# Stacking the high and low parts of prompt queries and keys by transfers inside SBUF

## The chip, the cores and the metric

One Trainium2 chip, one core of it, one launch. The metric is device time in microseconds (us) of one execution, as the median of the runs shown. The engines are PE (matrix products), DVE (vector), ACT (scalar, functions), POOL and SP; SP here only issues transfers, ACT issues some too.

## The reference

One inference step of a two-layer decoder on 1024 prompt tokens and eight samples of eight tokens. The change touches layer 0's differential attention on the prompt alone. There each of eight heads has two components (c) of 64 dimensions, with queries and keys normalised per component:

```python
q = rms_norm(zq.reshape(b, l, H_A, 2, DH_A), q_g) * (DH_A ** -0.5)
k = rms_norm(zk.reshape(b, l, H_A, 2, DH_A), k_g)
...
s = jnp.einsum('bqhcd,bkhcd->bhcqk', q, k).astype(jnp.float32)
bias = rel_bias[t5_bucket(q_pos[:, None] - k_pos[None, :])]
s = s + jnp.transpose(bias, (2, 0, 1)).astype(jnp.float32)[None, :, None]
...
p = jax.nn.softmax(s, axis=-1)
a = p[:, :, 0] - lam * p[:, :, 1]
return jnp.einsum('bhqk,bkhe->bqhe', a.astype(v.dtype), v)
```

Before it stands an input projection of 1024 to 7168 columns; after it, in the same layer, a spatial-gating branch and an output projection; then layer 1, a gated linear attention. All is float32 to within the tolerance of the comparison.

## The kernel before

The stage that the change is in runs over units, 8 heads (h) of 9 token blocks (i): eight prompt blocks of 128 tokens and one block of the 64 sample tokens. Its loop (lines 482 to 504) writes, for a step s, the work of several units at different ages: the projection `qkv_tile` of unit s, `qk_trans` of the unit two steps older, `scores` of the one five steps older, `av`, `av2` and `otrans` of still older ones. The order on each engine is not this one: the program is built with a scheduler that places every instruction by a modelled time line, within what the tiles' buffers and the dependences allow, and fixes the order engine by engine. On the chip each engine then runs its list in order, and an instruction that waits holds up those behind it on its engine.

Products in full precision are made from pairs: a value is rounded to a matmul format (the high part) and the difference to the value is the low part. For the projection three products are summed (lines 145 to 150), 24 matmuls of 384 columns for a prompt block; the 64 sample tokens stack both parts in one operand and need 16.

For the scores the same is done by stacking. `qk_trans` transposes a block's 128 columns of q and of k on PE into one PSUM tile `tp` (name qkt): its partitions 0 to 63 are component 0, 64 to 127 component 1. Per component c it then fills two SBUF tiles, `qs` (128 partitions; for c two sets of 128 columns, the high and the low part of q) and `ks` (128 partitions; for c the columns of four blocks). In `ks` the component's own 64 partitions hold the high part of k and the other 64 the low part; in `qs` both halves hold the same, the high part in the first set of columns and the low part in the second. So a score is two matmuls over 128 partitions in place of four over 64 (lines 391 to 396). `own` and `oth` are the component's own half and the other.

Before, DVE makes the high and low parts of q and k in five 64-partition steps per component, of which one, the copy of both q parts to the other half, is ACT's: 8 instructions on DVE and 2 on ACT for each unit. In the table PRM, 'qh': 'd' and 'kh': 'd' name DVE and 'qd': 'a' names ACT for these (line 92 is ACT's copy in the helper, lines 94 and 96 DVE's). 'qhb': 2 gives `qs` two buffers, 'ksb': 3 gives `ks` three, and 'qkb': 3 gives three to `qk`, the normalised rows that are transposed and, for k, also written out (line 354, on SP). The softmax has lines 402 to 415: DVE adds a bias band and takes the maximum, ACT exponentiates (409), DVE combines the components (415). Line 424 transposes the weights, line 431 multiplies them by v, lines 435 and 436 write and square the result on ACT, 443 transposes it (otp) and ACT stores that with a scale (oT). Transposes and v products share three PSUM buffers; the projection has one, which ACT empties into `qk` and `v`.

SP's queue carries the projection's weights (line 177, eight 192 KB loads per head into four buffers), the input rows, the key rows going out, one write per head of oT, and, once, sixteen small transfers of a bias table inside SBUF (line 232), in steps 20 to 27 of the loop as written.

Of the kernel before, what the change touches and what calls it, by code (L numbers as in the profile page):

```python
# [11 lines left out]
F32R = mybir.dt.float32r  # L12
I32 = mybir.dt.int32
AF = mybir.ActivationFunctionType
ALU = mybir.AluOpType
# [9 lines left out]
P = 128  # L25
KT = D // P
H = 8
DH = 64
# [6 lines left out]
TAU = 16.0  # L35
CH = ((0, 384), (384, 384), (768, 320))
NPRE = 8
PRM = {'ktc': 'a', 'ev': 'p', 'ekm': 'p', 'qem': 'd', 'gm': 2, 'wp': (3, 6), 'at': 'a', 'LQ': 2, 'LS': 5, 'LA': 6, 'L2': 8, 'LO': 12, 'on': 'a', 'oT': 'a', 'qk4': 'p', 'kh': 'd', 'vt': 'a', 'qkc': 'a', 'sq': 'p', 'kg': 'p', 'at0': 'a', 'at1': 'a', 'qh': 'd', 'onm': 'd', 'TS': True, 'p0': 2, 'p1': 2, 'qkb': 3, 'qhb': 2, 'ksb': 3, 'lpq': 2, 'qd': 'a', 'vb': 16, 'atb': 2, 'onb': 4}
ON = (0, 3, 6)
QB = 3  # L40
QE = 2
# [21 lines left out]
def rows(i):  # L63
    return P if i < NT - 1 else NS
# [12 lines left out]
def hybrid_step(  # L77
# [7 lines left out]
    nc = tc.nc  # L85
    pe, act, dve, pool = nc.tensor, nc.scalar, nc.vector, nc.gpsimd
# [3 lines left out]
    def cpy(e, o, i_, scale=None):  # L90
        if e == 'a':
            act.activation(o, i_, AF.Copy, scale=scale) if scale is not None else act.copy(o, i_)  # L92
        elif scale is not None:
            G[e].tensor_scalar_mul(o, i_, scale)
        else:
            G[e].tensor_copy(o, i_)

    def f32(a):
        return a.bitcast(F32)
# [88 lines left out]
    if True:  # L188
# [24 lines left out]
        def bias_setup(pp, ps, tb):  # L213
            rel = pp.tile([33, H], F32, name="rel", bufs=1)
            r31 = pp.tile([32, H], F32, name="r31", bufs=1)
            oh = pp.tile([33, 384], F32, tag="on", name="oh", bufs=PRM["onb"])
            dve.memset(rel[32:33, :], BIG)
# [5 lines left out]
            pe.matmul(bps[:H, :384], rel, oh, start=True, stop=True)  # L223
            bsb = pp.tile([H, 384], F32, tag="on", name="bsb", bufs=PRM["onb"])
            dve.tensor_copy(bsb, bps[:H, :384])
# [32 lines left out]
        with ExitStack() as p1:  # L258
            pa = p1.enter_context(tc.tile_pool(name="pa", bufs=2))
# [3 lines left out]
            kg = const([P, P], "kg")  # L263
            qg = const([P, 1], "qg")
# [5 lines left out]
            def small_consts():  # L270
                nc.sync.dma_start(kg, k_norm_g.rearrange("o c d -> o (c d)").broadcast_to([P, P]))
                nc.sync.dma_start(qg, q_norm_g.rearrange("o c d -> (o c d)")[:, None])
                nc.sync.dma_start(sg, subln_g.rearrange("o d -> d o"))
                lamt = pa.tile([P, 4, DH], F32, tag="p0", name="lamt", bufs=PRM["p0"])
                nc.sync.dma_start(lamt, lam.rearrange("o f d -> o (f d)").broadcast_to([P, 4 * DH]).rearrange("p (f d) -> p f d", f=4))
                nc.sync.dma_start(n1g, norm1_g.rearrange("o (k p) -> p (o k)", p=P))
                lamp = pa.tile([P, 2, DH], F32, tag="p0", name="lamp", bufs=PRM["p0"])
                lams = const([P, 2], "lams")
# [79 lines left out]
            def qk_trans(h, i, qk):  # L358
                r = rows(i)
                tp = ps.tile([P, 512], F32, tag="t", name=f"qkt{h}_{i}", bufs=3)  # L360
                pe.transpose(tp[:, 0:r], qk[:r, 0:128], ident[:r, :r])
                pe.transpose(tp[:, 128:128 + r], qk[:r, 128:256], ident[:r, :r])
                if i == NT - 1:
                    for c in range(2):
                        q8 = slice(c * DH, (c + 1) * DH)
                        act.activation(qbd[q8, h, :, h // 4, c, :], tp[q8, 0:NS].rearrange("p (b q) -> p b q", b=NB),
                                       AF.Copy, scale=qg[q8])
                    dve.tensor_copy(ksT[:, h, :], tp[:, 128:128 + NS])
                    return None
                qs = pa.tile([P, 2, 2, P], F32R, tag="qs", name=f"qs{h}_{i}", bufs=PRM["qhb"])  # L370
                if i % KW == 0:
                    kts[h, i // KW] = pa.tile([P, 2, KW * P], F32R, tag="ks", name=f"ks{h}_{i}", bufs=PRM["ksb"])
                ks = kts[h, i // KW]
                o = i % KW * P
                for c in range(2):
                    own, oth = slice(c * DH, (c + 1) * DH), slice((1 - c) * DH, (2 - c) * DH)
                    cpy(PRM['qh'], qs[own, c, 0], tp[own, 0:128], qg[own])
                    dve.scalar_tensor_tensor(qs[own, c, 1], tp[own, 0:128], qg[own], f32(qs[own, c, 0]), ALU.mult, ALU.subtract)  # L378
                    cpy(PRM['qd'], qs[oth, c], f32(qs[own, c]))
                    cpy(PRM['kh'], ks[own, c, o:o + P], tp[own, 128:256])  # L380
                    dve.tensor_tensor(ks[oth, c, o:o + P], tp[own, 128:256], f32(ks[own, c, o:o + P]), ALU.subtract)  # L381
                return (qs,)

            def scores(h, i, qs):
# [68 lines left out]
            wp = ps.tile([P, 512], F32, tag="t", name="wp", bufs=3)  # L453
# [28 lines left out]
            for s in range(len(units) + max(8, PRM['LO'] + 1)):  # L482
# [15 lines left out]
                if s < len(units):  # L498
                    h, i = units[s]
# [168 lines left out]
        with ExitStack() as p2:  # L668
            pb = p2.enter_context(tc.tile_pool(name="pb", bufs=1, reuse_waits="tile"))
            vb = [pb.tile([P, D], F32, name=f"vb{i}") for i in range(NT)]  # L670
# [218 lines left out]
    with ExitStack() as p4:  # L889
# [130 lines left out]
        for n, (c0, cw) in enumerate(CH):  # L1020
            tp = psd.tile([P, 512], F32, tag="x", name=f"rbp{n}", bufs=4)
            for q in range(3):
                i = n * 3 + q
# [390 lines left out]
        i = NT - 1  # L1414
# [5 lines left out]
        for n, i in enumerate(OO):  # L1420
            to = TO + PB * n + DO[n]
# [72 lines left out]
```

## Time and profile before

| | |
|---|---|
| median of 3 runs | 1789.59 us (1786.38 to 1795.03) |
| the profiled execution | 1789.87 us, its span 1788.1 us |
| PE busy | 1742.9 us, 97% of the span |
| DVE, ACT, POOL busy | 1006.3, 754.5, 605.6 us |
| transfers | 211.55 MB |

An engine's busy time is the union of its instructions' times. Matmuls overlap one another on PE, so their shown lengths add up to more than their pace. A row "x <- y L378: 2.2, 6, 0.6" in the waits says who waited for whom, for how many us in total, how often, and the longest. SP runs nothing but issues; its rows show how long an issue occupies the queue, and an arrow to a DMA on another engine's row shows when a transfer had landed for its reader.

### The profile page before, as it was taken

To read this page: it belongs to the slowest core of one execution; us is meant where nothing else is said; L and a number is where in the kernel's file an instruction comes from. 1 tells how busy PE (TensorE), PEld (TensorE's weight loads), DVE (VectorE), ACT (ScalarE), POOL (GpSimd) and SP (SyncE) were. 2 spreads that over 40 slices of the span, in tenths; PEclk is the share of its full clock that TensorE was granted. 3 is DMA by queue.
4 is the path that set the end of the run, shared out by engine and by line. 5 is a ranking of instruction groups with operands and counts; after the bars stand their busy time and mean duration, and the time that the engine had idled before them with its cause. 6 is when DMAs were issued, how large, how long until landed. Compare 5 with 4: busy or idle time off the path is not lost.

```text
span 1788.1 us, 31862 instructions
## 1 busy us (share of the span) xinstructions
PE 1742.9 (97%) x11437; PEld 1631.3 (91%) x11437; DVE 1006.3 (56%) x2231; ACT 754.5 (42%) x1934; POOL 605.6 (34%) x881
## 2 busy tenths in 40 slices
PE   8999999999999999999999999999899999998998
PEld 8898999999999888889999999999899999996777
DVE  6988988888892322324833442534265445667442
ACT  5666666665763222223222332423252334345241
POOL 5656655565653221011522100144012223235240
PEclk8999999999999999999999999999999999998999
DMA  7202211220223766747221362433134334438741
GB/s 212 59 20 75 68 42 45 68 67 19 67 71 121 244 218 216 242 142 221 72 77 60 109 188 74 134 94 92 59 121 144 101 119 125 129 116 264 239 127 71
DMA packets 223141, 211.55 MB, mean 118 GB/s; under 512 B 22253, under 2 KB 200982, under 8 KB 222982
## 3 DMA queue, kind: packets, MB, share of 16 engines
q1 hardware_dynamic: 203350, 194.29, 35.1%
q10 hardware_dynamic: 19632, 15.21, 2.8%
q8 instruction: 91, 1.49, 0.4%
q14 instruction: 68, 0.56, 0.1%
HBM read 151.29 MB, written 56.24 MB: 116 GB/s over the span
## 4 chain that ended last, share of the span: by engine, by line
PE 66%; DVE 15%; DMA 6%; ACT 5%; POOL 4%; issue 3%; SPq 0%; ACTq 0%; POOLq 0%; DVEq 0%
PE o L1371 5%; PE yo L148 3%; PE yo L150 3%; PE yo L149 3%; PE vg L148 3%; PE vg L149 3%; PE vg L150 3%; PE zv L148 2%; PE zu L148 2%; PE zv L149 2%; PE zv L150 2%; PE zu L150 2%; PE gb L148 2%; PE zu L149 2%; PE gb L149 2%
## 5 line engine op out<-in xcount | busy, mean ns | idle before, releaser
L409 ACT ACTIVATE p<-s,nm 128x256 f32<-128x256 f32 (+7 forms) x128 | 95.0, 747 | 44.5 <-DVE nm L406 26.1
L396 PE MATMUL s<-ks,qs 128*128 128x512 f32 (+3 forms) x384 | 95.6, 363 | 3.9 <-DVE ks L381 2.2
L92 ACT CAST qs<-qs 64x256 fp32r<-64x256 f32 x128 | 51.7, 404 | 83.5 <-DVE qs L378 77.6
L1118 POOL TENSOR_TENSOR e<-e,k 128x256 f32<-128x256 f32 (+1 forms) x50 | 42.2, 850 | 111.6 <-ACT e L1115 97.6
L396 PEld LDWEIGHTS s<-ks,qs 128*128 128x128 f32 x384 | 64.3, 189 | 14.3 <-ACT qs L92 3.8
L431 PE MATMUL o<-v,at 128*128 128x128 f32 x576 | 75.9, 277 | 1.4 <-ACT at L92 1.4
L136 POOL TENSOR_TENSOR s<-s,mhalf 128x4 f32<-128x4 f32 (+1 forms) x72 | 74.5, 1035 | 5.2
L335 POOL TENSOR_TENSOR sq<-qk 128x256 f32<-128x256 f32 (+1 forms) x72 | 47.8, 664 | 83.1 <-ACT qk L92 82.1
L431 PEld LDWEIGHTS o<-v,at 128*128 128x128 f32 x576 | 70.6, 192 | 4.0 <-ACT at L92 2.4
L834 DVE TENSOR_TENSOR yp<-yp,yo 128x384 f32<-128x384 f32 (+1 forms) x48 | 25.4, 530 | 75.6 <-ACT yp L833 41.7
L404 DVE TENSOR_REDUCE nm<-s 128x1 f32<-128x640 f32 (+3 forms) x64 | 65.2, 1019 | 1.1
L744 POOL TENSOR_TENSOR u<-u,th 128x384 f32<-128x384 f32 (+1 forms) x24 | 28.6, 1192 | 99.8 <-DVE th L743 99.3
L402 DVE TENSOR_TENSOR s<-s,tb 128x256 f32<-128x256 f32 (+1 forms) x128 | 52.5, 412 | 8.9 <-PE s L396 5.8
L415 DVE SCALAR_TENSOR_TENSOR p<-p,fac,p 128x128 f32<-128x128 f32 (+3 forms) x64 | 54.7, 854 | 1.6
L1371 PE MATMUL o<-w1h,oh 128*128 128x512 f32 x128 | 53.0, 414 | 1.2 <-ACT oh L1348 1.2
L92 ACT COPY at<-atp 128x512 f32<-128x512 f32 (+2 forms) x96 | 44.6, 480 | 14.7 <-PE atp L424 14.2
L1371 PE MATMUL o<-w1l,oh 128*128 128x512 f32 x128 | 50.8, 397 | 0.0
L1371 PE MATMUL o<-w1h,ol 128*128 128x512 f32 x128 | 50.3, 407 | 0.0
L743 DVE SCALAR_TENSOR_TENSOR th<-th,gb 128x384 f32<-128x384 f32 (+1 forms) x24 | 12.5, 526 | 65.3 <-ACT th L742 65.3
L424 PE MATMUL atp<-cf,p 128*128 128x128 f32 x288 | 46.7, 273 | 1.7 <-DVE p L415 1.4
L340 POOL TENSOR_TENSOR qk<-qk,s 128x256 f32<-128x256 f32 (+1 forms) x72 | 46.0, 638 | 4.5
L1115 ACT ACTIVATE e<-e 128x512 f32<-128x512 f32 (+1 forms) x50 | 31.1, 623 | 37.4 <-DVE e L1114 33.6
(819 smaller groups left out, 6344.2 us busy)
## 6 DMA issues: line engine op xcount, KB each, us to landing
kp<-in_cache_k SPq DMA_DIRECT2D x32, 512.0 KB
vp<-in_cache_v SPq DMA_DIRECT2D x32, 512.0 KB
or<-oT_d SPq DMA_DIRECT2D x16, 384.0 KB
vb_d<-zs SPq DMA_DIRECT2D x36, 128.0 KB
oT_d<-ob SPq DMA_DIRECT2D x8, 544.0 KB
gt<-g_d SPq DMA_DIRECT2D x34, 128.0 KB
xt<-in_x_prompt SPq DMA_DIRECT2D x8, 512.0 KB
out<-v ACTq DMA_DIRECT2D x64, 64.0 KB
```

What stands on the lines that cost most here:

```text
L92: act.activation(o, i_, AF.Copy, scale=scale) if scale is not None else act.copy(o, i_)
L136: pool.tensor_tensor(dst, dst, mhalf[:dst.shape[0], :n], ALU.pow)
L148: pe.matmul(out, lh, rh, start=(s == 0), stop=False)
L149: pe.matmul(out, lh, rl, start=False, stop=False)
L150: pe.matmul(out, ll, rh, start=False, stop=(s == n - 1))
L396: pe.matmul(sc[c][:, k0:k0 + w], qs[:, c, l], kts[h, j][:, c, :w], start=(l == 0), stop=(l == 1))
L402: dve.tensor_tensor(sc[c][:, lo:n], sc[c][:, lo:n], backwards(tb[:, h, 0:n - lo]), ALU.add)
L404: dve.tensor_reduce(nm[:, c:c + 1], sc[c][:, :n], axis=AX.X, op=ALU.max, negate=True)
L409: act.activation(pc[:, :n], sc[c][:, :n], AF.Exp, bias=nm[:, c:c + 1], accum_out=ss[:, c:c + 1])
L415: dve.scalar_tensor_tensor(pt[0][:, :n], pt[1][:, :n], fac, pt[0][:, :n], ALU.mult, ALU.add)
L431: pe.matmul(op[:, :P], at[:, j * P:(j + 1) * P], vts[h, j], start=(j == 0), stop=(j == i))
L1371: pe.matmul(it.mp[:r], lh[:, k, :r], rh[k][:, cs], start=(k == 0 and a == 0), stop=(k == KT - 1 and a == 2))
```

## The change

For a unit the PSUM tile is now written by instructions on all 128 partitions into one SBUF tile `sp`, which has one buffer: on ACT the scaled high part of q and the high part of k, on DVE both low parts. Then SP issues eight transfers inside SBUF, each on 64 partitions: for each component and each half of the partitions, one of 128 columns from `sp` to `ks` and one of 256 columns from `sp` to `qs`. `qk` has two buffers in place of three.

```diff
-PRM = {..., 'qkb': 3, 'qhb': 2, 'ksb': 3, ...}
+PRM = {..., 'qkb': 2, 'qhb': 2, 'ksb': 3, ...}
...
                 o = i % KW * P
+                sp = pa.tile([P, 2, 2, P], F32R, tag="sp", name=f"sp{h}_{i}", bufs=1)
+                act.activation(sp[:, 0, 0], tp[:, 0:128], AF.Copy, scale=qg)
+                act.copy(sp[:, 1, 0], tp[:, 128:256])
+                dve.scalar_tensor_tensor(sp[:, 0, 1], tp[:, 0:128], qg, f32(sp[:, 0, 0]), ALU.mult, ALU.subtract)
+                dve.tensor_tensor(sp[:, 1, 1], tp[:, 128:256], f32(sp[:, 1, 0]), ALU.subtract)
                 for c in range(2):
-                    own, oth = slice(c * DH, (c + 1) * DH), slice((1 - c) * DH, (2 - c) * DH)
-                    cpy(PRM['qh'], qs[own, c, 0], tp[own, 0:128], qg[own])
-                    dve.scalar_tensor_tensor(qs[own, c, 1], tp[own, 0:128], qg[own], f32(qs[own, c, 0]), ALU.mult, ALU.subtract)
-                    cpy(PRM['qd'], qs[oth, c], f32(qs[own, c]))
-                    cpy(PRM['kh'], ks[own, c, o:o + P], tp[own, 128:256])
-                    dve.tensor_tensor(ks[oth, c, o:o + P], tp[own, 128:256], f32(ks[own, c, o:o + P]), ALU.subtract)
+                    own = slice(c * DH, (c + 1) * DH)
+                    for u in range(2):
+                        to = slice(u * DH, (u + 1) * DH)
+                        nc.sync.dma_start(f32(ks[to, c, o:o + P]), f32(sp[own, 1, u]))
+                        nc.sync.dma_start(f32(qs[to, c]), f32(sp[own, 0]))
                 return (qs,)
```

The scheduler then places everything of the stage anew. Three places show how. In these rows qs5_1 is the tile of head 5, block 1, and so on; the last number only counts.

SP's queue before, in head 4, where the key rows of blocks 1 to 4 go out one after another (each row with the semaphores that it waits for):

```order
L354 DMA out_2<-qk4_1_3898 128x128 [waits DMAHW6_49,Activation_49,Pool_49]
L354 DMA out_2<-qk4_2_4001 128x128 [waits DMAHW0_49,Activation_49,Pool_49]
L354 DMA out_2<-qk4_3_4157 128x128 [waits DMAHW2_49,Activation_49,Pool_49]
L354 DMA out_2<-qk4_4_4241 128x128 [waits DMAHW4_49,Activation_49,Pool_49]
L354 DMA out_2<-qk4_5_4332 128x128 [waits DMAHW6_49,Activation_49,Pool_49]
```

SP's queue now, in head 5, between the key rows of blocks 2 and 3:

```order
L354 DMA out_2<-qk5_2_5017 128x128 [waits DMAHW4_49,Pool_49]
L384 DMA ks5_0_4978<-sp5_1_5090 64x128 [waits DMAHW6_49,Activation_49]
L384 DMA ks5_0_4978<-sp5_1_5090 64x128 [waits DMAHW7_49]
L385 DMA qs5_1_5089<-sp5_1_5090 64x256 [waits DMAHW0_49,DVE_49,PE_49]
L384 DMA ks5_0_4978<-sp5_1_5090 64x128 [waits DMAHW1_49,DVE_49]
L385 DMA qs5_1_5089<-sp5_1_5090 64x256 [waits DMAHW2_49]
L385 DMA qs5_1_5089<-sp5_1_5090 64x256 [waits DMAHW3_49]
L384 DMA ks5_0_4978<-sp5_1_5090 64x128 [waits DMAHW4_49]
L385 DMA qs5_1_5089<-sp5_1_5090 64x256 [waits DMAHW5_49]
L354 DMA out_2<-qk5_3_5176 128x128 [waits DMAHW6_49,Pool_49]
```

Between two key rows there are now the eight transfers of an older block; the first needs ACT's part only, the third DVE's and the score matmuls that last read this qs buffer.

ACT's list before, around block 1 of head 5:

```order
L92 CAST qs5_1_4966<-qs5_1_4966 64x256
L92 COPY qk5_3_5050<-qkv5_3_5025 128x256
L92 COPY v5_3_5060<-qkv5_3_5025 128x128
L92 ACTIVATE oT4_4908<-otp4_1_5064,sg_115 128x128
L355 DMA out_3<-v5_3_5060 128x128
L92 CAST qs5_1_4966<-qs5_1_4966 64x256
L92 ACTIVATE on4_5_5074<-o4_5_5067,rr4_5_4755 128x128
```

And now at the same block:

```order
L92 COPY v5_3_5186<-qkv5_3_5151 128x128
L92 ACTIVATE oT4_5031<-otp4_1_5190,sg_115 128x128
L376 ACTIVATE sp5_1_5090<-qkt5_1_5086,qg_114 128x128
L377 CAST sp5_1_5090<-qkt5_1_5086 128x128
L355 DMA out_3<-v5_3_5186 128x128
L92 ACTIVATE on4_5_5200<-o4_5_5193,rr4_5_4875 128x128
L440 ACTIVATE osq4_5_5201,ms4_5_5202<-o4_5_5193,rr4_5_4875 128x128
```

The two copies from DVE's parts have become two writes from PSUM, which stand together, behind the store of a transposed output and before the next output.

PE's list before, where head 5's scores of block 0 (second component) and block 1 (first component) stand, with the value products of head 4's block 5 between them:

```order
L396 MATMUL s_0_5167<-ks_0_4858,qs_0_4857 128x128 x2
L443 MATMUL otp_1_5064<-cf,on_1_4602 128x128
L431 MATMUL o_5_5067<-v_0_3812,at_5_4818 128x128
L431 MATMUL o_5_5067<-v_1_3908,at_5_4818 128x128
L431 MATMUL o_5_5067<-v_2_4011,at_5_4818 128x128
L431 MATMUL o_5_5067<-v_3_4167,at_5_4818 128x128
L431 MATMUL o_5_5067<-v_4_4251,at_5_4818 128x128
L431 MATMUL o_5_5067<-v_5_4342,at_5_4818 128x128
L396 MATMUL s_1_5263<-ks_0_4858,qs_1_4966 128x256 x2
```

And now there:

```order
L447 MATMUL otp_1_5190<-cf,on_1_4719 128x128
L400 MATMUL s_0_5296<-ks_0_4978,qs_0_4977 128x128 x2
L435 MATMUL o_5_5193<-v_0_3908,at_5_4938 128x128
L435 MATMUL o_5_5193<-v_1_4004,at_5_4938 128x128
L435 MATMUL o_5_5193<-v_2_4110,at_5_4938 128x128
L435 MATMUL o_5_5193<-v_3_4269,at_5_4938 128x128
L435 MATMUL o_5_5193<-v_4_4356,at_5_4938 128x128
L435 MATMUL o_5_5193<-v_5_4450,at_5_4938 128x128
L400 MATMUL s_0_5296<-ks_0_4978,qs_0_4977 128x128 x2
```

Block 0's two components now enclose the value products, and block 1's first stands behind the next projection; the transpose otp, on which ACT's store before sp5_1 waits, stands just ahead of block 0's scores.

## Rows read from the trace of the kernel before

**Rows 1.** The page: busy time by engine, and DVE in 40 slices, in tenths.

```profile
PE 1742.9 (97%) x11437; PEld 1631.3 (91%) x11437; DVE 1006.3 (56%) x2231; ACT 754.5 (42%) x1934; POOL 605.6 (34%) x881
DVE  6988988888892322324833442534265445667442
```

**Rows 2.** Busy time over five stretches, 50 to 550 us: their sum.

```profile
sum 500.00, PE 485.65 PEld 458.84 DVE 437.54 ACT 321.33 POOL 292.50; mean PE 97.13 PEld 91.77 DVE 87.51 ACT 64.27 POOL 58.50
```

**Rows 3.** Time line of PE in head 3: start, length, engine, line, operation, count.

```profile
251.99 0.38 PE L424 MATMUL atp<-cf,p 128*128 128x128 f32 x2
...
253.42 0.33 PE L148 MATMUL qkv<-wq3h,xh 128*128 128x384 f32 x1
253.59 0.33 PE L149 MATMUL qkv<-wq3l,xh 128*128 128x384 f32 x1
...
257.42 0.39 PE L431 MATMUL o<-v,at 128*128 128x128 f32 x2
```

**Rows 4.** Time line of ACT's queue: one issue per head, three heads apart.

```profile
325.97 0.50 ACTq L325 DMA_DIRECT2D sx<-st  x1
...
515.59 0.50 ACTq L325 DMA_DIRECT2D sx<-st  x1
```

**Rows 5.** Waits to 560 us on PE and its weight load; SP's over the span.

```profile
PE s L396 <- DVE ks L381: 2.2, 6, 0.6
...
PE qkt L361 <- DVE ks L381: 1.7, 4, 0.9
...
PEld s L396 <- ACT qs L92: 3.8, 7, 0.7
...
SPq L354 <- POOL qk L341: 272.1, 64, 5.7
```

**Rows 6.** Groups to 620 us: shapes, count, busy us, mean ns, idle before, releaser.

```profile
L404 DVE TENSOR_REDUCE nm<-s 128x1 f32<-128x640 f32 (+3 forms) x64 | 65.2, 1019 | 1.1
...
L378 DVE SCALAR_TENSOR_TENSOR qs<-qkt,qg,qs 64x128 fp32r<-64x128 f32 x128 | 44.5, 348 | 3.6
L94 DVE TENSOR_SCALAR qs<-qkt,qg 64x128 fp32r<-64x128 f32 x128 | 44.3, 346 | 1.9
L381 DVE TENSOR_TENSOR ks<-qkt,ks 64x128 fp32r<-64x128 f32 x128 | 36.9, 289 | 4.1
L96 DVE CAST ks<-qkt 64x128 fp32r<-64x128 f32 x128 | 36.1, 282 | 0.0
...
L94 DVE TENSOR_SCALAR on<-on,ms 128x128 f32<-128x128 f32 x64 | 25.3, 396 | 14.8 <-POOL ms L136 13.6
...
L92 ACT CAST qs<-qs 64x256 fp32r<-64x256 f32 x128 | 51.7, 404 | 83.5 <-DVE qs L378 77.6 <-DVE fac L414 3.6
...
L92 ACT ACTIVATE oT<-otp,sg 128x128 f32<-128x128 f32 x64 | 23.9, 377 | 0.6 <-PE otp L443 0.4
...
L92 ACT COPY v<-qkv 128x128 f32<-128x128 f32 x64 | 17.3, 271 | 0.1
```

**Rows 7.** Time line, later stages: 64-partition transfers inside SBUF and their readers.

```profile
1272.49 0.50 SPq L940 DMA_DIRECT2D vsx<-vst  x1
1274.65 0.51 DVE L954 TENSOR_TENSOR vst<-vst,vsx 64x344 f32<-64x344 f32 x1 [2.24 <-DMA vsx<-vst]
...
1732.55 0.48 ACTq L1367 DMA_DIRECT2D ysx<-yr  x1
1735.20 0.68 DVE L1379 TENSOR_TENSOR yr<-yr,ysx 64x512 f32<-64x512 f32 x1 [0.64 <-DMA ysx<-yr]
```

**Rows 8.** Time line of SP's queue in head 0: issues in a row are merged.

```profile
45.45 0.37 SPq L354 DMA_DIRECT2D out<-qk  x1
45.87 2.65 SPq L232 DMA_DIRECT2D biasS<-tb  x4
...
49.05 7.10 SPq L232 DMA_DIRECT2D biasS<-tb  x10
```

More of the change, by code (lines that the diff above doesn't have):

```diff
@@ L37 @@
 NPRE = 8
-PRM = {'ktc': 'a', 'ev': 'p', 'ekm': 'p', 'qem': 'd', 'gm': 2, 'wp': (3, 6), 'at': 'a', 'LQ': 2, 'LS': 5, 'LA': 6, 'L2': 8, 'LO': 12, 'on': 'a', 'oT': 'a', 'qk4': 'p', 'kh': 'd', 'vt': 'a', 'qkc': 'a', 'sq': 'p', 'kg': 'p', 'at0': 'a', 'at1': 'a', 'qh': 'd', 'onm': 'd', 'TS': True, 'p0': 2, 'p1': 2, 'qkb': 3, 'qhb': 2, 'ksb': 3, 'lpq': 2, 'qd': 'a', 'vb': 16, 'atb': 2, 'onb': 4}
+PRM = {'ktc': 'a', 'ev': 'p', 'ekm': 'p', 'qem': 'd', 'gm': 2, 'wp': (3, 6), 'at': 'a', 'LQ': 2, 'LS': 5, 'LA': 6, 'L2': 8, 'LO': 12, 'on': 'a', 'oT': 'a', 'qk4': 'p', 'kh': 'd', 'vt': 'a', 'qkc': 'a', 'sq': 'p', 'kg': 'p', 'at0': 'a', 'at1': 'a', 'qh': 'd', 'onm': 'd', 'TS': True, 'p0': 2, 'p1': 2, 'qkb': 2, 'qhb': 2, 'ksb': 3, 'lpq': 2, 'qd': 'a', 'vb': 16, 'atb': 2, 'onb': 4}
 ON = (0, 3, 6)
```

## The prediction

> **What bounds the kernel now.** I read the page first, then the stretches, the groups by line, the waits, and last the time lines of SP and PE. The page gives PE 97% and DVE 56% of the span [rows 1], but DVE's slices show two regimes: mostly eight or nine tenths in the first twelve, mostly two to four afterwards [rows 1]. The edited lines run only in that first part, eight heads of eight prompt blocks and one sample block. In its 500 us from 50 to 550 PE is busy 485.7, DVE 437.5 and ACT 321.3 [rows 2], so what PE can visibly get back there is 14.3 us. A little more is hidden in it, since matmuls overlap. Projection matmuls of 384 columns start 0.17 us apart (0.173 over a longer run; two of the starts stand in [rows 3]), though each is shown 0.33 long; two transposes take 0.38, the first of which ends at 0.27, so they start 0.11 apart, and so do the fp32 halves of the value product [rows 3]. One head has 208 projection matmuls (8 blocks of 24, and 16 of the sample block), 48 score matmuls on 18,432 columns, 62 transposes and 72 value-product records: 36.0 + 8.3 + 6.8 + 8.1 = 59.2 us. A head lasts (515.59 - 325.97)/3 = 63.2 us [rows 4]. So PE sets the pace of this stage, it loses 4.0 us per head or 32 in all, and that is the ceiling of any gain (1.8%). Of PE's visible waits, those ended by the lines under edit are 2.2 + 1.7 on PE and 3.8 on its weight load, 7.7 us [rows 5]. ACT waits 77.6 us for DVE inside the edited lines [rows 6], and that wait is not on PE's path.
>
> **What is removed.** Per block DVE loses two each of 346, 348, 282 and 289 ns: 2.53 us; ACT loses two of 404: 0.81 us [rows 6]. The new instructions work on 128 partitions with the same 128 columns. Rows nearby with 128x128 cost what 64x128 costs: the scaled write of the attention output 377 ns on ACT against 404 for 64x256, the value copy 271, and DVE's 128x128 scaling 396 against 346 [rows 6]. I take 0.38 + 0.27 = 0.65 us on ACT and 0.35 + 0.29 = 0.64 on DVE (the two subtracting rows as they stand). DVE saves 1.9 us per block, 121 us over 64 blocks, ACT 10 us. Both engines work beside PE, so this is worth only what PE waits for them: 7.7 us by the rows that name the chain, 32 at the ceiling. I take **-8**; the gain would come near the ceiling only if all of PE's other waits were DVE's too.
>
> **What is added.** SP issues eight transfers per block, 512 in all. No transfer of this shape stands in the trace. The nearest is L940: 64 partitions, inside SBUF, on SP; it occupies SP for 0.50 us and has landed 2.16 us after its start (1272.49 to the DVE instruction at 1274.65 that waits for it) [rows 7]. Its rows are 1,376 B long and the new ones 512 or 1,024 B. From ACT's queue a like one took 2.65 us to its reader (1732.55 to 1735.20) [rows 7]. SP needs about 0.05 more between two issues: four bias transfers, of 0.62 each, take 2.65 us, 0.66 apart [rows 8]. I take **0.55 us per issue and 2.1 us to landing**. The lower end is the 0.37 us of a 128-partition issue [rows 8], the upper the bias transfers' 0.66 [rows 8] with a landing of 2.65.
>
> There is one sp tile. So block n+1's first ACT write waits until all eight transfers of block n have landed, and a **ring** forms: ACT 0.65, about 0.1 to SP's first issue (it needs only ACT's key part; DVE's parts are ready while SP issues), seven pitches of 0.55 = 3.85 to the last issue, 2.1 to its landing, 0.15 back to ACT: 6.85 us. DVE's subtraction may stand behind a reduction, mean 1.02 us [rows 6]; part of that is hidden behind the first key issues, and I add 0.35: **7.2 us** per block. PE has 63.2/8 = 7.9 us per block on average, so the ring is hidden on average, but not in every block. From the changed order I add PE's own work from one block's first score matmul to the next's. Between blocks 0 and 1 of head 5 it is twenty-four projections 4.15, six value blocks of two records 1.34, eight transposes of the weights 0.87, three others 0.33, four score matmuls 0.45: 7.1 us. In the same way the eight steps of heads 4 to 7 are 8.1, 7.1, 8.4, 5.5, 8.7, 6.9, 7.0 and 7.5, together 59.2 as they must be. The ring exceeds them by 0.1 + 1.7 + 0.3 + 0.2 = 2.3 us; heads 1 to 3 have steps of 5.4 and 6.7, again 2.3. Seven heads give **+16**. This assumes that a long step doesn't lend its slack to a short one: the sp tile forbids ACT to run ahead.
>
> Three further costs are in SP's queue. The sixteen bias transfers (ten of them in 7.10 us, pauses included), 10.5 us in all [rows 8], now stand between the rings of heads 0 and 1; half of that is not hidden: **+5**. Eight weight loads per head, 128-partition issues of some 0.37 us each as the key row [rows 8], now stand between groups. SP's work per block is 8 x 0.55 + 0.37 = 4.8 of 7.9 us, so 3.1 us cover them, except where a load waits for its buffer and holds the next group; I take 0.5 us per head: **+3.5**. The outgoing key row waits 272.1 us for POOL in 64 issues, 4.3 each [rows 5], at no cost now because nothing behind it is urgent. Afterwards the next group stands behind it, but the row belongs to a block two later in the order and is ready while the group before it is being issued. Cost nothing; uncovered, up to 4.3 us a block. With two qk buffers in place of three, the copy two blocks later waits for that row's landing: ready within its own block (SP issues one per block [rows 5]) 7.9, the group ahead 4.4, issue and landing 2.1 to 2.7 make 14.4 to 15.0, and two blocks are 15.8: just hidden; uncovered, it costs what goes beyond. The transfers' 24 MB over 63.2 x 8 us are some 50 GB/s; no row says that this crowds the queues.
>
> Sum: -8 + 16 + 5 + 3.5 = +16.5 on the profiled execution's 1789.87 (span 1788.1 and 1.8 around it; 0.3 above the median), **1806 us**; by itself between 1794 and 1830.
>
> **Rivals.** *The ring is hidden and DVE's relief shows.* If slack does pass from long steps to short ones, or an issue costs 0.37, the ring is 0.65 + 0.1 + 7 x 0.42 + 2.1 + 0.15 = 5.9 us, under nearly every step. Then only some 4 us of the bias transfers are left against a relief of 8 to 24: around 1778. For it: DVE falls from 87% to about 63%, and PE's score matmul needs only the transfers of its own component, six of the eight issues in the order. Against it: that the issues are nearly two thirds of the ring. The Trainium skill ("DMA: Bandwidth & Descriptors", section "Issuing engines are not separate DMA queues") holds that the sequencer's time to initiate a transfer is usually small beside the transfer; with issues at nothing the ring would be 3.0 us and this rival the outcome. Here one issue of 0.50 stands beside 2.16 to landing [rows 7], and eight of them are 4.0: the rows speak against leaving it out, and I let the chance stand at 0.22.
>
> *The ring paces every block.* With 0.66 per issue and 2.65 to landing the ring is 0.65 + 0.1 + 4.65 + 2.65 + 0.15 + 0.35 = 8.6 us. Then every step but the 8.7 takes 8.6: 68.9 us per head, +9.7; seven heads 68, head 0 and the bias transfers 10, the loads 7, relief 8: 1867 us. It decides from a ring of about 8 us, above most steps. For it: the bias transfers, also inside SBUF and on SP, are this slow; each added semaphore wait costs too. Against it: L940 is nearer in shape and place. Chance 0.22.
>
> *The relief does not come, and the ring costs little.* Either 128 partitions cost more than 64 (the rows above speak against it), or PE's lost 32 us are others' waits, while the ring stays hidden: 1785 to 1797. Chance 0.12.
>
> **How the numbers follow.** The forecast has 0.44, of which 0.10 lies below +0.5%; the rivals have 0.22, 0.22 and 0.12. Some 0.5% (9 us) is about what a measurement can tell from no change. Faster 0.22, same 0.22, slower 0.56. For eight in ten the range must reach into both outer rivals: from 1774, the gain at twice the named waits, to 1867, where the long ring stands.
>
> **What would show it.** Right: DVE busy in 50 to 550 falls by some 110 us; SP's new issues last about 0.5 us; ACT's sp write waits for a DMA, and PE's score matmul begins to wait for transfers in short steps; a head lasts about 65 us. Wrong towards slow: issues of 0.6 or landings near 3 us, and PE waiting at every score matmul. Wrong towards fast: no wait for those transfers on PE and a head under 63 us. Everything after 600 us should keep its length; a difference there would be outside this account.

## The result and the profile after

The changed kernel takes 1818.26 us (median of 6, 1813.46 to 1821.60) against 1792.53 for the kernel before, measured beside it. The ratio is 1.0152, 95% interval 1.0133 to 1.0170: some 27 us slower. The profiled execution has a span of 1819.9 us, 31.8 above that of before.

First the page of the changed kernel (busy times, DVE's slices) and its stretch from 50 to 550, the rows that answer to [rows 1, 2]:

```profile
PE 1750.5 (96%) x11437; PEld 1628.8 (90%) x11437; DVE 898.2 (49%) x1847; ACT 729.4 (40%) x1934; POOL 608.6 (33%) x881
...
DVE  6656556657664232222943342444254455567442
```

```profile
sum 500.00, PE 474.58 PEld 443.21 DVE 316.24 ACT 283.60 POOL 285.14; mean PE 474.58 PEld 443.21 DVE 316.24 ACT 283.60 POOL 285.14
```

DVE has lost 121.3 us of this stretch and PE has not gained: it is busy 11.1 us less there, and gets less done in that time. The issue that stands once in each head, as in [rows 4], after the change:

```profile
141.02 0.56 ACTq L325 DMA_DIRECT2D sx<-st  x1
...
349.46 0.50 ACTq L325 DMA_DIRECT2D sx<-st  x1
...
540.92 0.50 ACTq L325 DMA_DIRECT2D sx<-st  x1
```

Heads 2 to 4 last (349.46 - 141.02)/3 = 69.5 us, heads 5 to 7 63.8. All eight issues, read the same way in both traces, give the place of the loss: the first comes 6.3 us later, the seven heads behind it take 464.5 in place of 445.6 (+19.0), and from the last issue to the last transposed output (otp) it is 57.7 in place of 52.6 (+5.1). That is 30.4 of the 31.8; from there to the end it is 1221.3 us against 1220.0.

Who waits: ACT's first write of sp (line 376) as its own group, with what ended its engine's idle time, and the new issues on SP (shortest, median and longest in ns):

```profile
L376 ACT ACTIVATE sp<-qkt,qg x64: 356/367/412, 33.6 to 556.0; 128x128 fp32r<-128x128 f32 x64
its engine sat idle before it (us, times) until:
  DMA qs<-sp: 29.7, 17
  DMA out<-qk: 12.6, 5
  DMA ks<-sp: 7.4, 3
```

```profile
L384 SPq DMA_DIRECT2D ks<-sp x256: 461/587/1969, 35.2 to 561.1; - x128
...
L385 SPq DMA_DIRECT2D qs<-sp x256: 461/588/2108, 35.8 to 562.2; - x128
```

And waits to 600 us, on SP and on PE (for whom, us in total, how often, the longest):

```profile
SPq L354 <- POOL qk L341: 19.0, 15, 3.0
...
SPq L385 <- DVE sp L378: 14.0, 21, 1.5
```

```profile
PE s L400 <- DMA qs<-sp: 5.1, 9, 1.2
PE qkv L148 <- ACT v L92: 4.9, 8, 1.8
PE qkt L361 <- ACT at L92: 4.2, 6, 1.3
```

ACT stands some 54 us at the sp write, 50 of them for landings. SP, which used to stand 272.1 us at the key rows [rows 5], now has 19.0 left there: it issues for 358.8 of the 500 us from 50 to 550, against 59.2 before. PE waits for the transfers themselves only 5.1 us. More of its waits name ACT: the copy of v that empties the projection's one PSUM buffer, and the copies that free the shared ones. These stand in ACT's list behind an sp write that waits. In the seven heads behind the first, PE's idle time that instructions of ACT ended is 11.0 us, against 4.6 before; that transfers ended, 4.1 against none.

### The profile page after: what moved, and what is told of

The parts are those of the page before. It is cut to its first block, busy times and chain, and to the rows that moved or that the text cites. A ratio compares the mean times of both kernels' runs of the same rounds, so it can differ in the third digit from the quotient of the medians.

```text
span 1819.9 us, 32754 instructions
## 1 busy us (share of the span) xinstructions
PE 1750.5 (96%) x11437; PEld 1628.8 (90%) x11437; DVE 898.2 (49%) x1847; ACT 729.4 (40%) x1934; POOL 608.6 (33%) x881
## 4 chain that ended last, share of the span: by engine, by line
PE 69%; DMA 10%; DVE 3%; ACT 3%; issue 3%; POOL 2%; SPq 2%; ACTq 0%; DVEq 0%; POOLq 0%
PE o L1375 5%; PE yo L148 3%; PE yo L150 3%; PE yo L149 3%; PE qkv L148 3%; PE qkv L150 3%; PE qkv L149 3%; PE vg L148 3%; DMA oT_d<-oTr 3%; PE vg L149 3%; PE vg L150 3%; PE o L435 2%; PE s L400 2%; PE zu L148 2%; PE zv L148 2%
## 5 line engine op out<-in xcount | busy, mean ns | idle before, releaser
L94 DVE TENSOR_SCALAR on<-on,ms 128x128 f32<-128x128 f32 x64 | 31.6, 493 | 42.5 <-POOL ms L136 41.8
L376 ACT ACTIVATE sp<-qkt,qg 128x128 fp32r<-128x128 f32 x64 | 23.7, 370 | 54.3 <-DMA qs<-sp 29.7
```

## One turn of the ring, clean and stretched

SP and ACT of the changed kernel in head 6, from one write of sp to the next:

```profile
446.18 0.37 ACT L376 ACTIVATE sp<-qkt,qg 128x128 fp32r<-128x128 f32 x1 [1.02 <-DMA qs<-sp]
...
453.21 0.37 ACT L376 ACTIVATE sp<-qkt,qg 128x128 fp32r<-128x128 f32 x1 [0.36 <-DMA qs<-sp]
```

```profile
446.73 1.10 SPq L384 DMA_DIRECT2D ks<-sp  x2
447.93 0.54 SPq L385 DMA_DIRECT2D qs<-sp  x1
448.56 0.55 SPq L384 DMA_DIRECT2D ks<-sp  x1
449.16 1.23 SPq L385 DMA_DIRECT2D qs<-sp  x2
450.43 0.59 SPq L384 DMA_DIRECT2D ks<-sp  x1
451.07 0.59 SPq L385 DMA_DIRECT2D qs<-sp  x1
```

The ring is 7.03 us: 0.55 from the write to the first issue, 4.34 from first to last issue (0.62 apart), 2.14 to ACT's next write. The forecast had 6.85 for a turn without DVE's delay. A little later:

```profile
475.63 0.37 ACT L376 ACTIVATE sp<-qkt,qg 128x128 fp32r<-128x128 f32 x1
...
484.09 0.37 ACT L376 ACTIVATE sp<-qkt,qg 128x128 fp32r<-128x128 f32 x1
```

```profile
476.18 1.11 SPq L384 DMA_DIRECT2D ks<-sp  x2
478.81 0.46 SPq L385 DMA_DIRECT2D qs<-sp  x1
479.37 0.55 SPq L384 DMA_DIRECT2D ks<-sp  x1
479.97 1.23 SPq L385 DMA_DIRECT2D qs<-sp  x2
481.24 0.59 SPq L384 DMA_DIRECT2D ks<-sp  x1
481.88 0.59 SPq L385 DMA_DIRECT2D qs<-sp  x1
```

Here SP stands idle from 477.29 to 478.81, before the first transfer that needs DVE's low part, which DVE began to write at 478.41 (the waits of these 4 us have SP 1.5 us behind that write), and the turn is 8.46. I laid all 63 intervals between sp writes out like this. In 45 of them the next write comes less than 2.8 us after the last issue, and I count these as ended by the ring; in 28 of the 45 ACT stood idle just before the write. Their mean is 7.9 us; 7.65 for the 38 with only the eight issues in them, 8.99 for the seven in which a weight load, a key row or a bias transfer stands between.

## The experiments

Theory: DVE's relief comes and is small; one sp tile makes a ring that paces most blocks; the rest is SP's queue. Rivals: the lost qk buffer, the new division of work between ACT and DVE itself, the transfers' bytes, single foreign issues in SP's queue. Each kernel was measured beside the kernel before on the same chip; the ratios are to it, with 95% intervals. Kernels of one group ran together, beside the same runs of the kernel before:

| group | kernel | us | ratio |
|---|---|---|---|
| 1 | bqk2: before, two qk buffers | 1786.23 | 1.0008 (0.9995–1.0021) |
| 1 | nostack: no transfers | 1777.48 | 0.9960 (0.9944–0.9976) |
| 1 | noring: transfers that nothing reads | 1792.31 | 1.0048 (1.0030–1.0066) |
| 1 | lean2: after, two sp tiles | 1798.08 | 1.0074 (1.0053–1.0094) |
| 2 | lean1: after, side tiles moved | 1812.92 | 1.0130 (1.0091–1.0170) |
| 2 | twoq: after, key transfers on ACT | 1837.06 | 1.0259 (1.0222–1.0296) |
| 2 | lean2b: lean2, bias on ACT | 1802.55 | 1.0069 (1.0041–1.0096) |
| 2 | qonly: queries alone | 1792.97 | 1.0021 (1.0001–1.0040) |
| 3 | lean2x: lean2, sample row on ACT | 1800.73 | 1.0061 (1.0044–1.0078) |
| 3 | lean3x: lean2x, three qk | 1787.46 | 0.9983 (0.9964–1.0003) |
| 3 | nrsmall: noring, 16 columns | 1801.58 | 1.0078 (1.0055–1.0101) |
| 3 | wact: after, weight loads on ACT, later stages' too | 1831.81 | 1.0245 (1.0201–1.0289) |
| 4 | lean1q3: lean1, three qk | 1809.83 | 1.0139 (1.0114–1.0164) |
| 4 | lean3: lean2, three qk | 1787.88 | 1.0021 (1.0005–1.0037) |
| 4 | nostack3: nostack, three qk | 1777.93 | 0.9958 (0.9940–0.9976) |
| 4 | noring3: noring, three qk, side tiles moved | 1785.01 | 0.9993 (0.9978–1.0009) |
| 5 | lean3x5: lean3x again | 1793.56 | 1.0036 (1.0019–1.0052) |
| 5 | qonly3: qonly, all remedies | 1790.29 | 1.0005 (0.9988–1.0022) |

lean3x and lean3x5 are one kernel, and their intervals don't meet. So the interval holds for a comparison within a group; between groups I don't read less than 0.5% (9 us). Within a group the order still differs from kernel to kernel: behind the last otp, where no edit but wact's reaches, the profiled executions take between 1213.2 and 1226.2 us, while the one kernel measured twice takes 1223.1 and 1222.7 there. So where a step of 5 or 6 us between two kernels stands has to be looked up in their traces.

### The lost qk buffer alone

```diff
 kernel before:
-'qkb': 3
+'qkb': 2
```

> The kernel before with two qk buffers in place of three, nothing else. If the lost buffer is what costs (the copy into qk two blocks later waits for the key row's landing), this alone is slower by a large part of after's 26 us, 1805 to 1818. If the transfers and their one sp tile are the cause, it stays within 4 us of before, 1789 to 1796.

1.0008: without transfers the third buffer is worth nothing.

### The relief alone, and with three buffers

```diff
 kernel after:
-sp = pa.tile(...)
-act.activation(sp[:, 0, 0], tp[:, 0:128], AF.Copy, scale=qg)
+act.activation(qs[:, 0, 0], tp[:, 0:128], AF.Copy, scale=qg)
 (the other three write qs[:, 0, 1], ks[:, 0, o:o + P], ks[:, 1, o:o + P])
-for c in range(2): ... (the eight dma_start)
...
-pe.matmul(..., qs[:, c, l], ...)
+pe.matmul(..., qs[:, 0, l], ...)
```

> After without sp and without the eight transfers: ACT and DVE write their four 128-partition results straight into qs and ks, and both components read the first component's qs. The stacking is left out, so the scores are others. This is the relief by itself. By the prediction's first term DVE is busy about 316 us of 50 to 550 and the time falls by 8 us, to 1785; at the ceiling (all that PE loses) it would be 1760; if the relief is worth nothing, 1792. If this is slower than before, the new split of the work between ACT and DVE is itself the cause and the transfers are not.

> No transfers and no sp tile, the stacking left out, with three qk buffers as before. If two buffers hold something back even without transfers, below 0.996 times before: 1768 to 1775. If the key row's way out is hidden as long as SP's queue is empty, the same 0.996: 1777 to 1782.

0.9960 and 0.9958: a gain of 7 to 7.5 us, with either number of qk buffers. The new division of work is not the cause. The stretch from 50 to 550 of the first of them, in which PE is busy 5.7 us more than in [rows 2] and DVE 113 less:

```profile
sum 500.00, PE 491.32 PEld 468.36 DVE 324.22 ACT 297.63 POOL 312.06; mean PE 491.32 PEld 468.36 DVE 324.22 ACT 297.63 POOL 312.06
```

Its seven heads behind the first take 434.0 us, 62.0 each; 59.2 is PE's own work by the prediction's count.

### The transfers without a reader

```diff
 kernel nostack:
+sc = pa.tile([P, 2, 2, P], F32, tag="sc", ..., bufs=1)
+for c in range(2):
+    for u in range(2):
+        nc.sync.dma_start(sc[to, 1, c], f32(ks[own, u, o:o + P]))
+        nc.sync.dma_start(sc[to, 0], f32(qs[own, 0]))
```

> As the last one, with the eight 64-partition transfers of each block put back on SP, in the same order and sizes, but from qs and ks into a scratch tile that nothing reads: SP issues as in after, the transfers use the same bytes, and neither ACT nor PE waits for them. It leaves out the stacking. If the ring (ACT's next write waiting for eight landings) is the cause, this is within 5 us of the kernel without transfers. If the time in SP's queue or the crowding of the transfer queues is the cause (weights and key rows late behind the issues), it is as slow as after, 1812 to 1820.

> Eight transfers a block into a scratch tile that nothing reads, the stacking left out, with three qk buffers. If the 15 us that these transfers cost are the key row standing behind them in SP's queue and the copy into qk waiting for it, they go to 3 or less: 1778 to 1784. If they are SP's other work (weights late), 1790 to 1796 as with two.

```diff
 kernel noring:
-        nc.sync.dma_start(sc[to, 1, c], f32(ks[own, u, o:o + P]))
-        nc.sync.dma_start(sc[to, 0], f32(qs[own, 0]))
+        nc.sync.dma_start(sc[to, 1, c, 0:16], f32(ks[own, u, o:o + 16]))
+        nc.sync.dma_start(sc[to, 0, 0, 0:16], f32(qs[own, 0, 0, 0:16]))
```

> The kernel whose eight transfers per block go into a scratch tile that nothing reads, with 16 columns in each transfer in place of 128 or 256: as many issues on SP, a tenth of the bytes. It leaves out the stacking. If the time that SP needs to issue is what costs 15 us there, it stays at 1.003 to 1.007 times before. If the bytes do (crowded transfer queues, contention for SBUF), it falls to the time of the kernel without transfers, 0.996.

Eight transfers that nobody reads cost 0.0088 or 16 us over nostack with two qk buffers, and 0.0035 or 6 us over nostack3 with three, each within one group. With 16 columns per transfer nothing comes back (1.0078). It is the number of issues, not the bytes. The rows of SP's issues in noring and in nrsmall show the same lengths for 256 and for 16 columns:

```profile
L385 SPq DMA_DIRECT2D sc<-qs x256: 461/587/1677, 35.0 to 528.7; - x128
```

```profile
L385 SPq DMA_DIRECT2D sc<-qs x256: 461/588/1639, 34.8 to 534.0; - x128
```

The scheduler places a kernel anew whenever an edit changes its modelled times, so nrsmall is not noring in every place of its order; its 0.003 more is no finding.

The cost doesn't come block by block. Six of noring's seven heads behind the first last 60.2 to 63.4 us, 370.4 together against 371.9 in nostack. Head 3 lasts 71.1 in place of 62.0 (its first and last row here), and the stretch from the last issue of sx to the last otp is 6.2 longer:

```profile
196.33 0.50 ACTq L325 DMA_DIRECT2D sx<-st  x1
...
267.48 0.49 ACTq L325 DMA_DIRECT2D sx<-st  x1
```

Eight of the sixteen bias transfers now stand in SP's queue in that head. Nrsmall and noring3 have eight there too, and their head 3 lasts 72.1 and 66.1. No run takes the bias transfers out of these kernels, so that they are the cause is a guess.

### Two sp tiles

```diff
 kernel after:
-st = pa.tile([P, 384], F32, tag="st", name=f"st{h}", bufs=1)
-sx = pa.tile([NS, 384], F32, tag="sx", name=f"sx{h}", bufs=1)
+sr = pa.tile([P, D], F32, tag="xt", name=f"sr{h}", bufs=2)
+st, sx = sr[:, 0:384], sr[:NS, 384:768]
...
-sp = pa.tile(..., tag="sp", ..., bufs=1)
+sp = pa.tile(..., tag="sp", ..., bufs=2)
```

> After with two sp tiles; the 2 KB a partition come from the sample block's two side tiles, which now stand in a tile that the input rows used. ACT may then write block n+1 while block n's transfers are under way. If the one sp tile is the cause, ACT's wait at the sp write goes from 42 us to under 10 and the time comes back to 1785 to 1797. If PE waits for the stacked parts themselves (the latency from ACT's write to the score matmul) or SP's queue is the bound, it stays above 1808.

The control has the first half of that diff alone:

> After with the sample block's two side tiles standing in the input rows' tile, and still one sp tile: the control for the kernel with two sp tiles, which had this beside the second tile. If moving the side tiles does nothing, 1.013 to 1.018 times before, some 1808 to 1818, and the second sp tile is then worth the whole 15 us; if the side tiles did it, some 1798.

And with 'qkb': 3 in each:

> After with its third qk buffer back (side tiles moved for the room), one sp tile. If the lost qk buffer costs by itself wherever the transfers stand in SP's queue, 12 us come back: some 1800. If the one sp tile holds ACT first, so that a third buffer only lengthens the queue behind it, nothing comes back: 1811 to 1816.

> Two sp tiles and three qk buffers, the sample's input row on SP as in after. If the third buffer was what mattered in the kernel with the moved row, 1784 to 1790. If the moved row was needed as well (head 0 long by 12), 1796 to 1800.

The control (1.0130) is no faster than after by more than groups differ, so the room is not the cause. Within one group and with three qk buffers the second sp tile brings 1.0139 down to 1.0021: 21 us. With two buffers it is 1.0130 or 1.0152 to 1.0074 over different groups, 10 to 14. ACT's wait at the sp write for the landings of the block before falls from 29.7 us to this in lean2 and in lean3:

```profile
ACT sp L376 <- DMA qs<-sp: 7.5, 2, 5.0
```

```profile
ACT sp L376 <- DMA qs<-sp: 8.4, 5, 4.7
```

In lean2 the seven heads behind the first last 436.7 us, 8.9 less than before: there the relief shows. Head 0 (to its issue of sx) ends at 83.9, against 70.0 before. SP of lean2 in that head, then PE and ACT's waits (40 to 80 us), and PE's clock in stretches of 4 us (busy PE, PEld, DVE, ACT, POOL, granted clock, DMA share, GB/s):

```profile
60.73 0.59 SPq L385 DMA_DIRECT2D qs<-sp  x1
61.37 0.59 SPq L291 DMA_DIRECT2D xt<-in_x_sample  x1
```

```profile
68.29 1.11 PE L306 MATMUL xtp<-cf,xn 64*128 64x64 f32 x8 [4.22 <-DVE xn L300]
```

```profile
ACT xn L297 <- DMA xt<-in_x_sample: 9.5, 1, 9.5
```

```profile
60.31 1.19 PE L400 MATMUL s<-ks,qs 128*128 128x512 f32 x2 [2.35 <-DMA qs<-sp]
```

```profile
56.00:60.00 4.00, 1.96 (x10) 1.36 (x9) 2.42 (x4) 0.00 (x0) 0.32 (x1) 1.00 0.32 82
60.00:64.00 4.00, 2.32 (x4) 1.00 (x4) 0.00 (x0) 0.00 (x0) 0.00 (x0) 0.52 0.47 126
...
72.00:76.00 4.00, 3.85 (x12) 3.85 (x13) 2.96 (x9) 2.13 (x8) 0.66 (x2) 0.50 0.29 74
76.00:80.00 4.00, 4.00 (x24) 3.92 (x23) 0.00 (x0) 1.02 (x5) 2.80 (x5) 0.84 0.34 86
```

The sample's input row, issued at 38.3 us before, goes out at 61.4, behind the transfers of four blocks. ACT waits 9.5 us for it and PE 4.2. PE had already stood 2.35 us for transfers, up to 60.31, and its granted clock (third figure from the right in the stretches) was down to 0.52 in the 4 us from 60: the lower of its two levels, 1.2 of 2.4 GHz. It stayed at 0.50 to 76.

### Single issues moved out of SP's queue

```diff
 kernel lean2 (lean2b):
-nc.sync.dma_start(biasS[r0:r0 + 8, :], ...)
+nc.scalar.dma_start(biasS[r0:r0 + 8, :], ...)
 kernel lean2 (lean2x; lean3x has 'qkb': 3 as well):
-nc.sync.dma_start(xt[:r], x_rows(i))
+(nc.scalar if i == NT - 1 else nc.sync).dma_start(xt[:r], x_rows(i))
```

> After with two sp tiles (side tiles moved) and the sixteen transfers of the bias table issued on ACT's queue in place of SP's. If SP's queue, full in heads 1 and 2 with those transfers between the blocks', is what is left of the loss, this gains 4 to 9 us on the kernel with two sp tiles alone: 1789 to 1794. If their place in SP's queue is hidden, it is the same as that kernel, 1798.

> After with two sp tiles (side tiles moved) and one more step: the sample tokens' input row, a single transfer, is issued on ACT's queue in place of SP's. In the kernel with two sp tiles that row went out at 61.4 us, behind 32 transfers of blocks, against 38.3 before, PE stood 4.2 us for it and ran at half the granted clock for some 16 us after; its heads 1 to 7 took 62.4 us against 63.7 before, and only head 0 was longer, by 13.9. If that one row is what is left of the loss, head 0 ends near 72 us and the time is 1785 to 1789. If head 0 is long for another reason (the first blocks' transfers themselves), it stays at 1796 to 1800.

> The last kernel with three qk buffers again. If the third buffer does nothing, as in the kernel before, the same as that one within 3 us. If the copy into qk waits for the key row, which goes out later in a full SP queue, 3 to 6 us faster: 1780 to 1784, below before.

> The kernel with two sp tiles, three qk buffers and the sample's input row on ACT's queue, once more in five rounds. If it is faster than before, the interval stays below 1, some 0.997; if the first reading was luck, 1.000 to 1.002.

Moving the bias transfers gave nothing on the whole (in lean2 they stand in heads 0 and 1; in lean2b, on ACT, head 0 ends 5.4 us later still). Moving the sample's row did what it should where it stands (head 0 ends at 72.7), but the time did not fall: the scheduler placed the heads behind it anew and they took 446.1 us in place of 436.7, and what lies behind the stage 1226.2 in place of 1219.7. That theory of the rest falls. The third qk buffer did bring something in this company: 1.0061 to 0.9983 within the group, though the same kernel later gave 1.0036. What it removes can be seen in the waits of ACT before the copy into qk, in lean2 and in lean3 (to 600 us). In the second, waits that the profile could put down to nothing are gone and the copy waits for its projection instead:

```profile
ACT qk L92 <- issue: 32.4, 35, 2.4
```

```profile
ACT qk L92 <- PE qkv L150: 37.3, 33, 3.3
```

I can't show that these waits were for the key row's landing: only two of lean2's seventy copies came within 2.6 us of the issue that would free their buffer.

### Transfers or weights from ACT's queue

```diff
 kernel after (twoq):
-nc.sync.dma_start(f32(ks[to, c, o:o + P]), f32(sp[own, 1, u]))
+nc.scalar.dma_start(f32(ks[to, c, o:o + P]), f32(sp[own, 1, u]))
 kernel after (wact):
-nc.sync.dma_start(raw[:, 0, :].rearrange(...), ...)
+nc.scalar.dma_start(raw[:, 0, :].rearrange(...), ...)
```

> After with the four key transfers of each block issued on ACT's queue, the four query transfers on SP's. By the ring account the four issues on SP take 1.9 us from first to last in place of 4.3, the ring falls from 6.9 to about 4.5 us, below every step of PE, and SP is busy 2.9 us per block in place of 5.4. ACT pays four issues per block, at some 0.05 to 0.5 us each. If an issue on ACT costs little: 1785 to 1797. If it costs ACT 0.5 (2 us per block, 32 us per head... of 63 with 36 busy before), ACT itself gets late and the time stays at 1800 to 1818. If neither ring nor SP's queue is the cause, nothing changes.

> After with the projection's weights loaded from ACT's queue in place of SP's, eight issues per head; still one sp tile. If these loads stretch the ring (rings that held a weight load were 7.5 to 11.7 us, those without 6.9 to 7.5), the mean ring falls from 7.9 towards 7.4 and some 10 to 20 us come back, less what ACT pays for 64 issues of 0.6 (38 us, on an engine that is busy 58%): 1800 to 1812. If the ring's own eight issues and landing are all, no gain, 1814 to 1825.

Both are slower than after. ACT of twoq:

```profile
261.77 0.37 ACT L92 COPY qk<-qkv 128x256 f32<-128x256 f32 x1
261.80 2.44 ACTq L384 DMA_DIRECT2D ks<-sp  x4
264.28 0.27 ACT L92 COPY v<-qkv 128x128 f32<-128x128 f32 x1 [2.13 <-DVE nm L410]
```

Four issues hold ACT for 2.44 us, and the copy of v, which frees the projection's PSUM buffer, follows the fourth within 0.04 us. (The profile doesn't count issues as busy and puts the idle time down to DVE's nm, which ended at 263.93.) The ring did shrink: 19 intervals are still ended by it, most of them 5 to 6 us long. Every head now takes 67 to 71.

Wact says little about this stage. The edited line serves later stages as well: it moved 160 loads, 96 of them behind 820 us. Its seven heads take 464.3 us, as in after (464.5); 9.3 of the 11.4 us that its profiled execution is longer lie behind the stage.

### Half the transfers

```diff
 kernel after (qonly; qonly3 with bufs=2, 'qkb': 3, side tiles and sample row moved):
-sp = pa.tile([P, 2, 2, P], F32R, ...)
+sp = pa.tile([P, 2, P], F32R, ...)
 (ACT's and DVE's writes of q into sp stay; k is made as in the kernel before)
 for c in range(2):
+    cpy(PRM['kh'], ks[own, c, o:o + P], tp[own, 128:256])
+    dve.tensor_tensor(ks[oth, c, o:o + P], tp[own, 128:256], f32(ks[own, c, o:o + P]), ALU.subtract)
+    nc.sync.dma_start(f32(qs[own, c]), f32(sp[own]))
+    nc.sync.dma_start(f32(qs[oth, c]), f32(sp[own]))
```

> Only the queries go through sp and four transfers a block; the keys' parts are made by DVE's four 64-partition instructions as before. One sp tile. The ring has four issues: 0.4 + 0.1 + 3 x 0.62 + 2.0 + 0.35 = 4.7 us, under every step of PE, and SP's queue is busy 2.9 us of 7.9 per block. By the ring account with SP's queue there is then next to no cost, and about half of DVE's relief: 1780 to 1790. If each transfer costs by itself, whether or not a ring or a full queue stands behind it (a landing that PE waits for, crowding of the transfer queues), half of after's loss is left, 1795 to 1805.

> Only the queries through sp and four transfers a block, the keys' parts by DVE as before; two sp tiles, three qk buffers, the sample's input row on ACT's queue. By the terms measured so far: half of the relief of 7.5 us is -4, half of what transfers cost in SP's queue (6) is +3, and the wait of scores for them (5 with eight transfers) +2: 1.000 to 1.001. If what transfers cost comes with a full SP queue alone, it is about gone with four: 0.998.

With one sp tile and two qk buffers, four transfers per block cost next to nothing, 1.0021 in place of 1.0152: ACT's waits for landings at the sp write are 8.1 us where they were 50. With all remedies it is 1.0005. No form of the change was measured clearly faster than the kernel before: the lowest, lean3x, has 0.9983 with an interval that reaches 1.0003, and 1.0036 the second time.

## Why the prediction was right and wrong

Forecast 1806, range 1774 to 1867, slower the likeliest. Measured 1818 beside 1793. The direction, the mechanism and its place were right; the sum was 16.5 where some 27 came, and 31.8 in the profiled execution. By the four kernels of the fourth group, each with three qk buffers, the steps are: relief -7.5 (nostack3), transfers in SP's queue +6.3 (noring3 over it), the same transfers read, through two sp tiles, +5.0 (lean3 over that), one sp tile +21.1 (lean1q3 over that): 1.0139 in all, against 1.0152 for after, as measured in another group.

**Relief, -8: right.** -7.1 and -7.5. DVE lost 121.3 us of 50 to 550, where 121 was worked out over all 64 blocks; the 128-partition instructions last 367, 258, 350 and 280 ns, as the nearby rows had it [rows 6]. That 121 us of DVE were worth 7.5 was read from three rows of waits [rows 5].

**The ring, +16: the right mechanism, too small.** This is the term that was mis-sized. 21 over lean3 and 26 over noring3, with three qk buffers; in the heads behind the first, 464.5 - 436.7 = 28 against lean2. The clean turn was right within 3%. The step that failed is "7.2 us per block" as one length for all: the mean of the 45 turns that set the pace is 7.9. SP's issue takes 0.59 (pitch 0.62), not 0.50 (0.55), which is half a microsecond in seven pitches, and issues of 0.6 were the prediction's own sign of an error towards slow; DVE's part comes later than the 0.35 allowed for when it stands behind a reduction; and the weight loads, key rows and bias transfers, which the sum priced as terms of their own, lengthen the turn they stand in. By the prediction's own steps a ring of 7.9 would make a head 64.7, 38 us in all: more than was measured. So the rule that every excess adds in full is too strict as well. Either a long step lends slack to a short one, or the ring covers part of what PE loses in any case (a head lasts 62.1 in nostack3, beside 59.2 of its own work); no run tells the two apart. A turn taken too short and a rule too strict work against each other, and that 16 came as near as it did is in part luck. The mean turn lies midway between the forecast's 7.2 and the 8.6 of the rival in which the ring paces every block.

**SP's queue, +5 and +3.5: about the size, the reason open.** Transfers without a reader cost 6 us, 16 with two qk buffers. Eight issues at 0.62 are 5 of the 7.9 us of a block, and that by itself costs nothing in most heads of noring. The loss stands in single places: the head that holds half of the bias transfers, and the end of the stage. In after itself, where they stand in heads 0 and 1 as the forecast had it, head 1 is 1.7 us shorter than before. In lean2 taking the bias transfers off SP's queue gave nothing, and no run moves the weight loads of this stage alone. What stands urgent behind the transfers can pay, as the sample's row did in lean2. In the Trainium skill, "DMA: Bandwidth & Descriptors", section "Issuing engines are not separate DMA queues", a second issuing engine only saves the sequencer's time to initiate, usually small beside the transfer. Here an issue takes 0.59, with 16 columns as with 256, and from the last issue of the clean turn to ACT's next write, which waits for its landing, it is 2.14. The trace disagrees with "small" for transfers of this size, and on ACT that time is the engine's own, 2.44 us for four.

**PE's wait for the transfers, not in the sum.** The prediction named it as something to be seen and gave it no price. In after it is 5.1 us, and it goes with the one sp tile. The 5.0 by which lean3 is longer than noring3 is something else, as lean3's waits of PE to 600 us show:

```profile
PE xtp L306 <- DVE xn L300: 6.3, 3, 5.0
```

```profile
PE s L400 <- DMA qs<-sp: 1.7, 4, 0.8
```

Lean3's heads 1 to 7 are shorter than noring3's (430.8 us against 436.2), and its head 0 is 7.1 longer: the sample's row goes out at 61.9 us, behind 32 transfers, as in lean2, and PE stands 5.0 us for it. In after that row goes out at 45.1, behind eight, so this loss is not among after's in that size. The ring therefore has to bear about all that lean1q3 has over noring3, 26 us (heads 1 to 7: 436.2 to 462.3).

**Two qk buffers "just hidden": right for this kernel, for want of anything to uncover them.** Giving the third back brings nothing while one sp tile paces the blocks (1.0130 to 1.0139, in different groups). With the ring gone it is worth something between 4 and 14 us: the second bottleneck stood behind the first. Which wait inside SP's queue it removes stays open, and so does how much of it is a kinder order.

**The place.** Heads 1 to 7 lose 19.0, head 0 6.3 and the end of the stage 5.1, next to nothing after it (1221.3 against 1220.0): as forecast. Not foreseen: heads 2 to 4 lose 6 each and 6 and 7 next to nothing. In all of them the ring ends most of the blocks, so its length doesn't tell these heads apart; the order differs between them, and no run isolates that. The granted clock doesn't explain it: in heads 1 to 7 it falls below 0.95 only from 152 to 156 us (0.57) and from 296 to 304 (0.91, 0.66), in head 3 nowhere. "PE waiting at the scores" was the smaller part; more of it reaches PE through ACT, which stands blocked at the sp write with PE's copies in its list behind it. The second sp tile takes both away: in heads 1 to 7, PE's idle time that ACT ended falls from 15.1 us in lean1q3 to 2.2 in lean3, that transfers ended from 4.7 to 0.2. How each single late copy follows from a blocked write was not traced.

## What to carry to other kernels

A staging tile with one buffer between an engine and a group of transfers is a loop: the engine's write, as many issue pitches as there are transfers, one landing. Add what else the issuing queue carries to the turn itself, and compare the mean turn, not the clean one, with the time per block; then look at who stands behind the blocked write in that engine's list. What a relieved engine is worth is what the critical engine waits for it (here 7.5 us for 121), and half as many transfers may cost next to nothing where the full number costs 27 us.

## What the runs showed of the hardware

- An issue on SP of a 64-partition transfer inside SBUF takes 0.46 to 0.48 us when the queue was idle and 0.59 back to back, 0.62 from start to start, with 16, 128 or 256 columns; from the last issue to ACT's next write it was 2.14 in the clean turn.
- The same issue on ACT takes as long (median 607 ns) and stops ACT's instructions: four of them 2.44 us, and the kernel went from 1.0152 to 1.0259.
- In lean2's first head PE stood 2.35 us, its granted clock was 0.52 in the next 4 us, and with little work in between it stayed at 0.50 for some 16.
- The same kernel measured twice beside the kernel before gave 0.9983 and 1.0036, each with an interval of 0.002: an interval within a group of runs doesn't cover the difference between groups.
